# Rotary embedding: one signed sine product over eight positions on GpSimd, and one kind of TensorE tile

## Chip, cores and metric

The kernel runs on one core of a Trainium2 chip. The metric is the device time of one execution in microseconds (us). Times come from unprofiled runs. The profile is one more execution, recorded by the hardware profiler; its span, from the first to the last instruction, is a little shorter than the time.

## The reference

```python
batch, seq_len, n_heads, d_head = 8, 2048, 8, 64          # x is float32, 33.6 MB
def reference(x, cos, sin):                               # cos, sin: [2048, 32]
    x1 = x[..., :32]
    x2 = x[..., 32:]
    cos = cos[None, :, None, :]
    sin = sin[None, :, None, :]
    out1 = x1 * cos - x2 * sin
    out2 = x1 * sin + x2 * cos
    return np.concatenate([out1, out2], axis=-1)
```

Every row of 64 numbers (one head at one position) is split into halves of 32. Each half is multiplied by the cosines of its position, and to it is added the *other* half times the sines, with a minus sign for the first half. So out = x * cos + swap(x) * (-sin, +sin).

## The kernel before

A batch is laid out as 128 partitions with 16 positions each; a position is 8 heads of 64 numbers, that is HD = 512 elements. A batch is 4 MB in SBUF, there are five such buffers, and results are written in place before they are stored. The work goes in tiles of four positions (UNIT = 2048 elements), with halves of that at the very start and end. There are three kinds of tile:

- A: GpSimd multiplies by the sines (two instructions, one per half), VectorE multiplies by the cosines and adds.
- B: the same products, but TensorE adds them in PSUM, by multiplying both with the identity, and ScalarE copies the sum out.
- C: VectorE makes both products, without GpSimd; TensorE adds them (with the negative identity for the sign).

```python
    t1_pool = ctx.enter_context(tc.tile_pool(name="t1p", bufs=1, space=PSUM))
    o_pool = ctx.enter_context(tc.tile_pool(name="op", bufs=1, space=PSUM))
    t1s_pool = ctx.enter_context(tc.tile_pool(name="t1s", bufs=2))
    xpool = ctx.enter_context(tc.tile_pool(name="xpool", bufs=NBUF))     # NBUF = 5
    t2_pool = ctx.enter_context(tc.tile_pool(name="t2p", bufs=3))
    # ... tables: cos_sb, sin_sb, nsin in SBUF, cos_ps, sin_ps in PSUM ...
    for b, kind in ((1, "C"), (2, "B"), (3, "C"), (4, "B"), (5, "B")):
        kinds[(b, 0)] = kind                     # first tile of the batch; all others are "A"

    def rotate(b, lo, n):
        # ... t1 in PSUM for kind A, in SBUF (t1s) for B and C; t2 in SBUF ...
        if kind != "C":
            for u, tab in ((1, sin_sb), (0, nsin)):
                keep(nc.gpsimd.tensor_mul(
                        out=t2u[:, :, u, :].rearrange("p (r h) d -> p r h d", h=H),
                        in0=xu[:, :, 1 - u, :].rearrange("p (r h) d -> p r h d", h=H),
                        in1=rep(tab[:, r0 : r0 + nr, :], H)))
        keep(nc.vector.tensor_mul(out=t1..., in0=xk, in1=rep(cos_ps[...], 2 * H)))
        if kind == "A":
            keep(nc.vector.tensor_add(out=xt, in0=t1, in1=t2))
        elif kind == "B":
            for j in range(n // (2 * C)):        # C = 512
                o = o_pool.tile([P, 2 * C], f32, tag="o")
                for k in range(2):
                    # ... cs, oc: 512 columns of the tile and of o ...
                    nc.tensor.matmul(oc, eye, t1[:, cs], start=True, stop=False)
                    nc.tensor.matmul(oc, eye, t2[:, cs], start=False, stop=True)
                keep(nc.scalar.copy(xt[:, 2 * j * C : 2 * (j + 1) * C], o))
        else:
            # ... kind C: a second VectorE product with sin_ps, matmuls with eye and neye ...

    def pieces(b):
        if b == 0:    return [2 * HD, 2 * HD, UNIT, UNIT, UNIT]
        if b == last: return [UNIT, UNIT, UNIT, 2 * HD, 2 * HD]
        return [UNIT] * 4
    def shares(b):                               # what one store covers
        if b == 0:    return [HD, 7 * HD, 2 * UNIT]
        if b == last: return [2 * UNIT, UNIT, UNIT]
        return [ROW]
    # for each batch: rotate the pieces, store each share when it is done, then load batch b + 5
```

Loads are issued from the SyncE queue and stores from the ScalarE queue; those of the last batch go through SyncE too.

Of the kernel before, what the change touches and what calls it, by code (L numbers as in the profile page):

```python
# [9 lines left out]
@with_exitstack  # L10
def kernel(
    ctx: ExitStack,
    tc: tile.TileContext,
    x: bass.AP,
    cos: bass.AP,
    sin: bass.AP,
    out: bass.AP,
):
    nc = tc.nc
    keep = tc.keep_in_program_order  # L20
    f32 = mybir.dt.float32
    PSUM = bass.MemoryType.PSUM

    B, S, H, D = x.shape
    Dh = D // 2
    P = 128
    HD = H * D
    R = S // P
    ROW = R * HD
    UNIT = 4 * HD  # L30
    NBUF = 5
    C = 512
    last = B - 1

    xv = x.rearrange("b (q r) h d -> b q (r h d)", q=P)
    ov = out.rearrange("b (q r) h d -> b q (r h d)", q=P)
    cos_src = cos.rearrange("(q r) d -> q r d", q=P)
    sin_src = sin.rearrange("(q r) d -> q r d", q=P)

    const_pool = ctx.enter_context(tc.tile_pool(name="const", bufs=1))  # L40
    tab_pool = ctx.enter_context(tc.tile_pool(name="tab", bufs=1, space=PSUM))
    t1_pool = ctx.enter_context(tc.tile_pool(name="t1p", bufs=1, space=PSUM))
    o_pool = ctx.enter_context(tc.tile_pool(name="op", bufs=1, space=PSUM))
    t1s_pool = ctx.enter_context(tc.tile_pool(name="t1s", bufs=2))
    xpool = ctx.enter_context(tc.tile_pool(name="xpool", bufs=NBUF))
    t2_pool = ctx.enter_context(tc.tile_pool(name="t2p", bufs=3))

    cos_sb = const_pool.tile([P, R, Dh], f32, tag="cb")
    sin_sb = const_pool.tile([P, R, Dh], f32, tag="sb")
    nsin = const_pool.tile([P, R, Dh], f32, tag="ns")  # L50
    eye = const_pool.tile([P, P], f32, tag="eye")
    neye = const_pool.tile([P, P], f32, tag="neye")
    cos_ps = tab_pool.tile([P, R, Dh], f32, tag="cp")
    sin_ps = tab_pool.tile([P, R, Dh], f32, tag="sp")

    xts = {}

    def spans(sizes):
        lo = 0
        for n in sizes:  # L60
            yield lo, n
            lo += n

    def load(b):
        xt = xpool.tile([P, ROW], f32, tag="xt", name=f"xt{b}")
        for lo, n in spans([UNIT, UNIT, 2 * UNIT] if b == 0 else [ROW]):
            keep(nc.sync.dma_start(out=xt[:, lo : lo + n], in_=xv[b, :, lo : lo + n]))  # L67
            if b == 0 and lo == 0:
                keep(nc.sync.dma_start(out=cos_sb, in_=cos_src))  # L69
                keep(nc.sync.dma_start(out=sin_sb, in_=sin_src))  # L70
        xts[b] = xt

    def store(b, lo, n):
        queue = nc.sync if b == last else nc.scalar
        keep(queue.dma_start(out=ov[b, :, lo : lo + n], in_=xts[b][:, lo : lo + n]))  # L75

    for b in range(NBUF):
        load(b)

    nc.gpsimd.memset(eye, 0.0)  # L80
    nc.gpsimd.affine_select(
        out=eye,
        in_=eye,
        compare_op=mybir.AluOpType.not_equal,
        fill=1.0,
        base=0,
        pattern=[[-1, P]],
        channel_multiplier=1,
    )
    keep(nc.scalar.mul(nsin, sin_sb, -1.0))  # L90
    keep(nc.scalar.copy(sin_ps, sin_sb))  # L91
    keep(nc.scalar.mul(neye, eye, -1.0))
    keep(nc.vector.tensor_copy(cos_ps, cos_sb))  # L93

    def rep(a, n):
        return dataclasses.replace(a, ap=[a.ap[0][:], a.ap[1][:], [0, n], a.ap[-1][:]])

    kinds = {}
    for b, kind in ((1, "C"), (2, "B"), (3, "C"), (4, "B"), (5, "B")):
        kinds[(b, 0)] = kind  # L100

    def rotate(b, lo, n):
        kind = kinds.get((b, lo), "A")
        xt = xts[b][:, lo : lo + n]
        r0 = lo // HD
        nr = n // HD
        xk = xt.rearrange("p (r k d) -> p r k d", r=nr, d=Dh)
        xu = xt.rearrange("p (g u d) -> p g u d", u=2, d=Dh)
        if kind == "A":
            t1 = t1_pool.tile([P, n], f32, tag="t1")  # L110
        else:
            t1 = t1s_pool.tile([P, n], f32, tag="t1s")
        if kind == "C":
            t2 = t1s_pool.tile([P, n], f32, tag="t1s")
        else:
            t2 = t2_pool.tile([P, n], f32, tag="t2")
        t1u = t1.rearrange("p (g u d) -> p g u d", u=2, d=Dh)
        t2u = t2.rearrange("p (g u d) -> p g u d", u=2, d=Dh)
        if kind != "C":
            for u, tab in ((1, sin_sb), (0, nsin)):  # L120
                keep(
                    nc.gpsimd.tensor_mul(  # L122
                        out=t2u[:, :, u, :].rearrange("p (r h) d -> p r h d", h=H),
                        in0=xu[:, :, 1 - u, :].rearrange("p (r h) d -> p r h d", h=H),
                        in1=rep(tab[:, r0 : r0 + nr, :], H),
                    )
                )
        keep(
            nc.vector.tensor_mul(  # L129
                out=t1.rearrange("p (r k d) -> p r k d", r=nr, d=Dh),  # L130
                in0=xk,
                in1=rep(cos_ps[:, r0 : r0 + nr, :], 2 * H),
            )
        )
        if kind == "A":
            keep(nc.vector.tensor_add(out=xt, in0=t1, in1=t2))  # L136
        elif kind == "B":
            for j in range(n // (2 * C)):
                o = o_pool.tile([P, 2 * C], f32, tag="o")
                for k in range(2):  # L140
                    cs = slice((2 * j + k) * C, (2 * j + k + 1) * C)
                    oc = o[:, k * C : (k + 1) * C]
                    nc.tensor.matmul(oc, eye, t1[:, cs], start=True, stop=False)  # L143
                    nc.tensor.matmul(oc, eye, t2[:, cs], start=False, stop=True)  # L144
                keep(nc.scalar.copy(xt[:, 2 * j * C : 2 * (j + 1) * C], o))  # L145
        else:
            keep(
                nc.vector.tensor_mul(  # L148
                    out=t2.rearrange("p (r k d) -> p r k d", r=nr, d=Dh),
                    in0=xk,  # L150
                    in1=rep(sin_ps[:, r0 : r0 + nr, :], 2 * H),
                )
            )
            G = C // Dh
            for u in range(2):
                o = o_pool.tile([P, n // 2], f32, tag="o")
                for j in range(n // 2 // C):
                    oc = o[:, j * C : (j + 1) * C]
                    gs = slice(j * G, (j + 1) * G)
                    nc.tensor.matmul(oc, eye, t1u[:, gs, u, :], start=True, stop=False)  # L160
                    nc.tensor.matmul(  # L161
                        oc, eye if u else neye, t2u[:, gs, 1 - u, :], start=False, stop=True
                    )
                keep(
                    nc.scalar.copy(  # L165
                        xu[:, :, u, :], o.rearrange("p (g d) -> p g d", d=Dh)
                    )
                )

    def pieces(b):  # L170
        if b == 0:
            return [2 * HD, 2 * HD, UNIT, UNIT, UNIT]
        if b == last:
            return [UNIT, UNIT, UNIT, 2 * HD, 2 * HD]
        return [UNIT] * 4

    def shares(b):
        if b == 0:
            return [HD, 7 * HD, 2 * UNIT]
        if b == last:  # L180
            return [2 * UNIT, UNIT, UNIT]
        return [ROW]

    for b in range(B):
        done = 0
        outs = list(spans(shares(b)))
        for lo, n in spans(pieces(b)):
            rotate(b, lo, n)
            done = lo + n
            while outs and sum(outs[0]) <= done:  # L190
                store(b, *outs.pop(0))
        if b + NBUF <= last:
            load(b + NBUF)
# [30 lines left out]
```

## Time and profile before

| | |
|---|---|
| time, median of 3 runs | 163.48 us (163.35 to 163.52) |
| span of the profile | 161.6 us |
| VectorE busy | 140.1 us (87%), 66 instructions |
| GpSimd busy | 139.0 us (86%), 70 instructions |
| TensorE busy | 47.2 us (29%), 80 matmul passes |
| ScalarE busy | 12.8 us (8%) |
| moved by DMA | 67.65 MB, 419 GB/s over the span |

Busy time counts the stretches in which an engine worked; it does not say that the engine set the time. For that one reads which wait ended last: the profile notes, for each idle stretch of an engine, what released it, and it follows the work that ended last back through its releasers (the chain). "L122" is line 122 of the kernel: GpSimd's products are on L122, VectorE's cosine products on L129 and its adds on L136, the matmuls of kind B on L143 and L144 and their copies on L145. Queue q1 is that of SyncE, q10 that of ScalarE. In a line of the timeline, the first number is the start and the second the length in us; the brackets hold the idle time before, and what ended it.

### The profile page before, as it was taken

How to read it: one execution, taken by the hardware profiler on the slowest of the kernel's cores; microseconds unless marked ns; L12 is line 12 of the kernel's file. 1: busy time of each engine (PE TensorE's matmuls, PEld its weight loads, DVE VectorE, ACT ScalarE, POOL GpSimd, SP SyncE). 2: the span in 40 equal slices, each digit the busy share in tenths (PEclk: the TensorE clock that was granted, in tenths of full speed). 3: DMA queues.
4: the chain of work that ended last, by engine and by line, in shares of the span. 5: the costliest groups of instructions: out<-in, count | busy, mean ns of one | idle time of the engine just before them, and what ended most of it. 6: DMA issues, size and time to landing. Idle time of an engine off the chain costs nothing.

```text
span 161.6 us, 460 instructions
## 1 busy us (share of the span) xinstructions
PE 47.2 (29%) x80; PEld 17.8 (11%) x80; DVE 140.1 (87%) x66; ACT 12.8 (8%) x14; POOL 139.0 (86%) x70
## 2 busy tenths in 40 slices
PE   0000000497208760878029752972000000000000
PEld 0000000133003210222014211330000000000000
DVE  0468899999999999999999999999899998999900
ACT  3200000002200220021000220022000000000000
POOL 1299999999999899999996999998999969999200
PEclk9999999999965997599855998799555555555555
DMA  5999998899999999999999999999999999999995
GB/s 183 414 442 467 424 472 373 373 430 503 398 389 454 454 454 389 471 438 389 471 438 389 454 456 389 446 454 398 446 448 406 446 446 406 446 446 430 385 414 215
DMA packets 3458, 67.65 MB, mean 419 GB/s; under 512 B 384, under 2 KB 384, under 8 KB 768
## 3 DMA queue, kind: packets, MB, share of 16 engines
q1 hardware_dynamic: 2160, 38.27, 55.8%
q10 hardware_dynamic: 1296, 29.36, 42.2%
q14 instruction: 2, 0.02, 0.0%
HBM read 34.08 MB, written 33.55 MB: 419 GB/s over the span
## 4 chain that ended last, share of the span: by engine, by line
DMA 46%; DVE 37%; POOL 9%; issue 2%; SPq 1%; DVEq 0%; POOLq 0%; ACTq 0%
DMA xt<-in_x_dram 24%; DVE t L129 18%; DMA out_dram<-xt 18%; DVE xt L136 17%; POOL t L122 9%; DMA sin_sb<-in_sin_dram 3%; DVE t L148 1%; SPq L69 0%; SPq L67 0%; DVEq L136 0%; POOLq L122 0%; ACTq L75 0%
## 5 line engine op out<-in xcount | busy, mean ns | idle before, releaser
L122 POOL TENSOR_TENSOR t<-xt,sin_sb 128x1024 f32<-128x1024 f32 (+1 forms) x32 | 70.5, 2204 | 10.8 <-DMA sin_sb<-in_sin_dram 5.8
L129 DVE TENSOR_TENSOR t<-xt,cos_ps 128x2048 f32<-128x2048 f32 (+1 forms) x34 | 73.4, 2166 | 0.8
L122 POOL TENSOR_TENSOR t<-xt,nsin 128x1024 f32<-128x1024 f32 (+1 forms) x32 | 70.5, 2203 | 0.0
L136 DVE TENSOR_TENSOR xt<-t,t 128x2048 f32<-128x2048 f32 (+1 forms) x29 | 62.2, 2144 | 6.1 <-POOL t L122 3.7
L143 PE MATMUL o<-t,eye 128*128 128x512 f32 x24 | 16.5, 778 | 23.7 <-DVE t L129 20.2
L160 PE MATMUL o<-t,eye 128*128 128x512 f32 x16 | 10.6, 749 | 39.1 <-DVE t L129 36.9
L144 PE MATMUL o<-t,eye 128*128 128x512 f32 x24 | 14.7, 701 | 0.0
L145 ACT COPY xt<-o 128x1024 f32<-128x1024 f32 x6 | 6.1, 1012 | 45.7 <-PE o L144 45.7
L143 PEld LDWEIGHTS o<-t,eye 128*128 128x128 f32 x24 | 5.3, 244 | 32.8 <-issue 26.8
L160 PEld LDWEIGHTS o<-t,eye 128*128 128x128 f32 x16 | 3.6, 247 | 44.5 <-POOL t L122 30.6
L165 ACT COPY xt<-o 128x1024 f32<-128x1024 f32 x4 | 4.0, 1012 | 47.1 <-PE o L161 47.1
L144 PEld LDWEIGHTS o<-t,eye 128*128 128x128 f32 x24 | 5.7, 239 | 8.0 <-issue 8.0
L93 DVE COPY cos_ps<-cos_sb 128x512 f32<-128x512 f32 x1 | 0.7, 695 | 6.3 <-DMA cos_sb<-in_cos_dram 6.3
L161 PE MATMUL o<-t,neye 128*128 128x512 f32 x8 | 6.0, 847 | 0.2 <-DVE t L148 0.2
L148 DVE TENSOR_TENSOR t<-xt,sin_ps 128x2048 f32<-128x2048 f32 x2 | 4.6, 2279 | 0.0
L161 PE MATMUL o<-t,eye 128*128 128x512 f32 x8 | 4.1, 592 | 0.0
L161 PEld LDWEIGHTS o<-t,neye 128*128 128x128 f32 x8 | 1.8, 251 | 4.3 <-issue 2.7
L161 PEld LDWEIGHTS o<-t,eye 128*128 128x128 f32 x8 | 1.5, 190 | 1.9 <-issue 1.9
L90 ACT ACT_TABLE_LOAD x1 | 1.3, 1283 | 0.7 <-PEq L208 0.7
L90 ACT ACTIVATE nsin<-sin_sb 128x512 f32<-128x512 f32 x1 | 0.6, 630 | 5.0 <-DMA sin_sb<-in_sin_dram 5.0
L91 ACT COPY sin_ps<-sin_sb 128x512 f32<-128x512 f32 x1 | 0.6, 579 | 0.0
L80 POOL MEMSET eye<- 128x128 f32 x1 | 0.2, 205 | 0.3 <-POOLq L208 0.3
(6 smaller groups left out, 1.0 us busy)
## 6 DMA issues: line engine op xcount, KB each, us to landing
xt<-in_x_dram SPq DMA_DIRECT2D x7, 4096.0 KB, 39.0
out_dram<-xt ACTq DMA_DIRECT2D x6, 4096.0 KB, 28.3
xt<-in_x_dram SPq DMA_DIRECT2D x2, 1024.0 KB, 6.1
xt<-in_x_dram SPq DMA_DIRECT2D x1, 2048.0 KB, 11.5
out_dram<-xt ACTq DMA_DIRECT2D x1, 2048.0 KB, 25.3
out_dram<-xt SPq DMA_DIRECT2D x1, 2048.0 KB, 12.3
out_dram<-xt SPq DMA_DIRECT2D x2, 1024.0 KB, 8.7
out_dram<-xt ACTq DMA_DIRECT2D x1, 1792.0 KB, 20.2
```

Source lines behind the costliest of these rows:

```text
L90: keep(nc.scalar.mul(nsin, sin_sb, -1.0))
L93: keep(nc.vector.tensor_copy(cos_ps, cos_sb))
L122: nc.gpsimd.tensor_mul(out=t2u[:, :, u, :].rearrange("p (r h) d -> p r h d", h=H), in0=xu[:, :, 1 - u, :].rearrange("p (r h) d -> p r h d" ...
L129: nc.vector.tensor_mul(out=t1.rearrange("p (r k d) -> p r k d", r=nr, d=Dh), in0=xk, in1=rep(cos_ps[:, r0 : r0 + nr, :], 2 * H),)
L136: keep(nc.vector.tensor_add(out=xt, in0=t1, in1=t2))
L143: nc.tensor.matmul(oc, eye, t1[:, cs], start=True, stop=False)
L144: nc.tensor.matmul(oc, eye, t2[:, cs], start=False, stop=True)
L145: keep(nc.scalar.copy(xt[:, 2 * j * C : 2 * (j + 1) * C], o))
L148: nc.vector.tensor_mul(out=t2.rearrange("p (r k d) -> p r k d", r=nr, d=Dh), in0=xk, in1=rep(sin_ps[:, r0 : r0 + nr, :], 2 * H),)
L160: nc.tensor.matmul(oc, eye, t1u[:, gs, u, :], start=True, stop=False)
L161: nc.tensor.matmul(oc, eye if u else neye, t2u[:, gs, 1 - u, :], start=False, stop=True)
L165: nc.scalar.copy(xu[:, :, u, :], o.rearrange("p (g d) -> p g d", d=Dh))
```

## The change

The sine product becomes one GpSimd instruction instead of two: its first operand reads the two halves of each row in reversed order (a step of -32), and its second operand is a table `sgn` that holds -sin and +sin side by side for each position. One such instruction covers eight positions (4096 elements) in most batches, two to eight in the first, eight or four in the last. VectorE then works in tiles of four positions as before. Kind C is gone: in batches 1 to 5 the first four positions are added by TensorE in the manner of kind B, and all sine products are made by GpSimd. This needs fewer instructions and one code path, and takes two products off VectorE. The buffers change with it: t2 has two buffers of eight positions where it had three of four, t1s one buffer where it had two, and the negative identity and the sine table in PSUM are gone.

```diff
-    t1s_pool = ctx.enter_context(tc.tile_pool(name="t1s", bufs=2))
+    t1s_pool = ctx.enter_context(tc.tile_pool(name="t1s", bufs=1))
-    t2_pool = ctx.enter_context(tc.tile_pool(name="t2p", bufs=3))
+    t2_pool = ctx.enter_context(tc.tile_pool(name="t2p", bufs=2))
 ...
+    loads = {0: [4, 4, 8]}
+    products = {0: [2, 2, 4, 8], last: [8, 4, 4]}
+    stores = {0: [1, 7, 8], last: [8, 4, 4]}
+    on_tensor = {(b, 0) for b in range(1, 6)}
 ...
-    keep(nc.scalar.mul(nsin, sin_sb, -1.0))
-    keep(nc.scalar.copy(sin_ps, sin_sb))
-    keep(nc.scalar.mul(neye, eye, -1.0))
+    for lo, hi in ((0, 4), (4, R)):
+        keep(nc.scalar.mul(sgn[:, lo:hi, 0, :], sin_sb[:, lo:hi, :], -1.0))
+        keep(nc.scalar.copy(sgn[:, lo:hi, 1, :], sin_sb[:, lo:hi, :]))
 ...
+    def sine_product(b, lo, n):
+        xt = xts[b][:, lo * HD : (lo + n) * HD]
+        t2 = t2_pool.tile([P, n * HD], f32, tag="t2")
+        swapped = dataclasses.replace(
+            xt, offset=xt.offset + Dh,
+            ap=[xt.ap[0][:], [HD, n], [D, H], [-Dh, 2], [1, Dh]])
+        s = sgn[:, lo : lo + n, :, :]
+        signed = dataclasses.replace(
+            s, ap=[s.ap[0][:], [D, n], [0, H], [Dh, 2], [1, Dh]])
+        keep(nc.gpsimd.tensor_mul(out=t2..., in0=swapped, in1=signed))
+        return t2
 ...
+    def finish(b, lo, n, t2):
+        # ... t1 in SBUF (t1s) for tiles on_tensor, else in PSUM; cosine product as before ...
+        if (b, lo) not in on_tensor:
+            keep(nc.vector.tensor_add(out=xt, in0=t1, in1=t2))
+            return
+        # ... matmuls with eye and ScalarE copies exactly as in kind B ...
 ...
     for b in range(B):
-        for lo, n in spans(pieces(b)):
-            rotate(b, lo, n)
+        for lo, n in spans(products.get(b, [8, 8])):
+            t2 = sine_product(b, lo, n)
+            for at, m in spans([min(T, n)] * (n // min(T, n))):        # T = 4
+                finish(b, lo + at, m, t2[:, at * HD : (at + m) * HD])
 ...
```

## The prediction

> **What bounds the kernel now.** I began with the page's queue lines, because GpSimd at 86% and VectorE at 87% look like the limit and need not be.
>
> ```profile
> DMA packets 3458, 67.65 MB, mean 419 GB/s; under 512 B 384, under 2 KB 384, under 8 KB 768
> q1 hardware_dynamic: 2160, 38.27, 55.8%
> q10 hardware_dynamic: 1296, 29.36, 42.2%
> ```
>
> The two queues, loads and stores, together fill 98% of the 16 DMA engines' span of 161.6 us. The table of stretches of the span shows that this is true of every stretch but the first and the last (columns: stretch, length, then busy time of PE, PE load, VectorE, ScalarE, GpSimd, the granted clock, DMA share, GB/s):
>
> ```profile
> 0.00:5.00 5.00, 0.00 (x0) 0.00 (x0) 0.00 (x0) 1.28 (x1) 0.70 (x6) 1.00 0.64 218
> 5.00:45.00 40.00, 9.63 (x16) 3.49 (x16) 35.65 (x19) 3.38 (x5) 37.91 (x19) 1.00 1.01 429
> 125.00:155.00 30.00, 0.00 (x0) 0.00 (x0) 26.86 (x14) 0.00 (x0) 24.21 (x13) 0.50 0.99 427
> 155.00:162.00 7.00, 0.00 (x0) 0.00 (x0) 0.00 (x0) 0.00 (x0) 0.00 (x0) 0.50 0.65 275
> ```
>
> From 5 to 155 us the DMA share is about 1.00 at 427 to 435 GB/s. The chain of work that ended last agrees: in its middle it leaves the engines (columns: start, length, what):
>
> ```profile
> 63.12 29.40 DMA out_dram<-xt
> ...
> 92.59 39.11 DMA xt<-in_x_dram
> ...
> 131.83 4.63 POOL t L122 x2
> ...
> 152.18 1.22 DVE xt L136
> ```
>
> A store of batch 2 and the load of batch 7, which needs that store's buffer, hold 68.5 us of it. The last add ends at 153.4 us, the last 1 MB store is issued there and lands 7.3 us later, as older stores are still queued in front. So the kernel is bound by DMA, but VectorE and GpSimd are only a few us behind: a slowdown of theirs soon shows, a speedup hardly.
>
> **What the Trainium skill says.** DMA: Bandwidth & Descriptors (Specifications) gives a fabric ceiling of 435 GB/s; the trace's 427 to 435 in long stretches agrees. GPSIMD Engine Reference (3.1, Elementwise) puts a two-input operation at about 2.6 cycles per element at 1.2 GHz plus a dispatch per instruction: 2.17 ns per element; the trace gives 2.11 (below). SBUF — State Buffer (Who interferes with whom) says a VectorE instruction with at most one SBUF input does not contend with GpSimd; here the cosines and t1 of the adding tiles lie in PSUM, and GpSimd's spacing is 1.21 us at 8.32 with VectorE mostly idle and 1.20 at 9.53 with it at work: agreed, and unchanged by the change. TensorE: Matmul & The Clock Gate (What's actually happening) says the array starts at half clock and is let go after some 3.4 us of work; in this trace pairs of passes go from 2.04 to 1.02 us within a tile, each time anew.
>
> **The costs, from the timeline.** GpSimd, by the distance of starts:
>
> ```profile
> 8.32 1.25 POOL L122 TENSOR_TENSOR t<-xt,nsin 128x512 f32<-128x512 f32 x1
> 9.53 1.26 POOL L122 TENSOR_TENSOR t<-xt,sin_sb 128x512 f32<-128x512 f32 x1
> 46.27 2.33 POOL L122 TENSOR_TENSOR t<-xt,nsin 128x1024 f32<-128x1024 f32 x1
> 48.57 2.32 POOL L122 TENSOR_TENSOR t<-xt,sin_sb 128x1024 f32<-128x1024 f32 x1
> ```
>
> 512 elements take 1.21 us, 1024 take 2.28 (11.95 to 14.23) to 2.30 us. The slope is 1.08 us per 512 elements, which is one position, and the fixed part 0.13 us. One instruction over n positions then costs 0.13 + 1.08 n: 2.29 for two, 4.45 for four, 8.77 for eight. Four positions cost 4.58 today in two instructions. The new operand order walks the same runs of 32 elements on x, so I keep the slope.
>
> VectorE: an added tile of four positions has its pitch in the chain (product at 23.64, add at 26.04, before that add at 21.32): 2.40 + 2.32 = 4.72 us. A cosine product for a TensorE tile alone takes 2.2 us.
>
> One TensorE tile, first matmul to the second copy out:
>
> ```profile
> 100.06 2.04 PE L143 MATMUL o<-t,eye 128*128 128x512 f32 x2 [4.82 <-DVE t L129]
> ...
> 105.42 1.01 ACT L145 COPY xt<-o 128x1024 f32<-128x1024 f32 x1 [9.14 <-PE o L144]
> ...
> 110.23 1.01 ACT L145 COPY xt<-o 128x1024 f32<-128x1024 f32 x1 [3.79 <-PE o L144]
> ```
>
> TensorE lets go of t2 when the second copy starts: 10.2 us after its first matmul here, 10.0 in batch 2 (49.12 to 59.16), 11.5 in batch 4 (83.81 to 95.27); mean 10.6.
>
> **The change part by part.**
> - GpSimd's arithmetic. Before: 30 tiles of four positions, two of them in halves, 28 x 4.58 + 2 x 4.84 = 137.9 us; two more (batches 1 and 3) had their sine product on VectorE. After: all 32. Batch 0: 2.29 + 2.29 + 4.45 + 8.77 = 17.8; batches 1 to 6: 12 x 8.77 = 105.2; batch 7: 8.77 + 2 x 4.45 = 17.7. Sum 140.7, so +2.8 us: fewer instructions save about 6.4, the two tiles taken over cost 9.
> - VectorE loses two sine products and their second tiles (4.4 us) and the split of the last tile (0.5). Per batch from 1 to 5 it needs 2.2 + 3 x 4.72 = 16.4 us against GpSimd's 17.5, so it is off the path there; in batches 0, 6 and 7 it needs 18.9 and is on it.
> - Grain. An add can start only when a whole instruction is done: 8.77 us instead of 4.6 after the start of the product.
> - Buffers. Three t2 buffers of four positions become two of eight. The next but one product must wait until TensorE has let go of its tile. Call F the end of that product. GpSimd asks for the buffer at F + 8.77. VectorE finishes the group before (add, product, add) 7.0 after that group's end and then the cosine product, 2.2: about F + 0.5 without a stall, earlier by s after a stall of s. TensorE needs 10.6 from there, so it is done near F + 11.2 - s, and the new stall is 2.4 - s. This swings about 1.2 us, once for each of batches 2 to 6: 6.0 us.
> - Setup. The signed table takes two ScalarE passes after sine lands at 6.97, some 0.3 us each for four positions (the pass over 128x128 took 0.30): the first product starts at about 7.65 instead of 7.09.
>
> **The sum.** Batch 6 starts on GpSimd at 7.65 + 17.8 + 10 x 8.77 + 6.0 = 119.2 (before: 112.33). Its first product is done at 127.9 (first add before: 116.97). Then eight tiles of four on VectorE without a gap: 7 x 4.72 + 2.3 = 35.3, so the last add ends at 163.2 (before 153.4). Loads do not hold this up: before, x of batches 4 to 7 landed by 73.1, 92, 112.3 and 131.8, and here those batches start near 80, 100, 119 and 137. Stores: those of batches 1 to 5 go out 4 to 11 us later than before, DMA runs dry towards the end, and the last 1 MB store then takes about 5 us (the first 1 MB load took 4.9 with an empty queue). 168.2, plus 0.8 to the end of the span (as before, 160.8 to 161.6), plus the 1.9 us by which the time exceeds the span (163.48 against 161.6): 170.9. I take a little off for starts that overlap by about 0.1 us and predict **170.0 us**, 4.0% slower.
>
> **The rivals.**
> - DMA stays the bound and swallows it all: about 163.5. For it: the queues are full today, and no byte changes. Against: only some 5 us of the last store's wait is slack, and the sum adds 10 us at the last add. Faster by 2% would mean a span of about 158.3, and 67.65 MB at 435 GB/s take 155.5 without the 1.8 us before the first packet and the last receipt; nothing in the change speeds up a transfer.
> - TensorE's hold on t2 never stalls GpSimd, since its first matmul runs before the product is done or the clock is up early: the 6.0 goes, 164.9, within 2%. For it: the margin is small (10.6 against 8.77 + 0.5). Against: no tile before took under 10.0 us.
> - The long instruction has another rate. The reversed pair of halves and the zero step in one pattern have no example in this trace. 5% more per element is 0.43 us for each of sixteen groups, about 7 us, partly in place of the stalls: 174 to 177. If 5% less, VectorE and TensorE take over and it ends near 166.
> - VectorE's relief (4.9 us) decides: it would if it were the limit in the middle. It waited 3.7 us for GpSimd in all, so it was near it, but the product work moves to GpSimd, which becomes the slower of the two.
>
> **Range and chances.** Stalls of 0.5 to 2.0 us per batch instead of 1.2 move the end by -3.5 to +4.0, and the GpSimd rate by 2% moves it by about 3: 165.5 to 174.5. The line of 2% is at 166.75; only the first two rivals lie under it. Faster 0.03, same 0.22, slower 0.75.
>
> **What would show it.** GpSimd instructions over 4096 elements starting 8.7 to 8.9 us apart; a wait of GpSimd of 1 to 2 us before the first product of batches 2 to 6, put down to TensorE or the ScalarE copies; batch 6 starting near 119; VectorE without gaps from 128 to 163; the DMA share falling clearly under 1 after about 130 us, and the last store landing in about 5 us. Wrong would be: GpSimd without such waits, a first add of batch 6 before 122, or DMA still at 1.00 to the end.

## The result and the profile after

The changed kernel takes 195.24 us (194.78 to 196.25, 6 runs) against 163.49 us (163.35 to 163.68, 6 runs) for the kernel before, run beside it: a ratio of 1.195 (95% interval 1.191 to 1.198). The prediction was 170.0 us, in a range of 165.5 to 174.5: the direction was right, and the loss is almost five times the one predicted. In what follows, ratios leave disturbed runs out, so they can differ a little from the quotient of two medians.

The page of the changed kernel, its queue lines:

```profile
DMA packets 3457, 67.64 MB, mean 350 GB/s; under 512 B 384, under 2 KB 384, under 8 KB 768
q1 hardware_dynamic: 2160, 38.27, 47.5%
q10 hardware_dynamic: 1296, 29.36, 35.7%
```

The bytes are the same, but the queues fill only 83% of the span, where they filled 98%. The table of stretches (columns as in the prediction) says where the rest went. First the kernel before between 85 and 125 us, then the changed kernel:

```profile
85.00:125.00 40.00, 18.07 (x32) 6.78 (x30) 38.36 (x18) 4.05 (x4) 37.63 (x17) 0.76 1.00 431
...
85.00:125.00 40.00, 15.52 (x26) 5.28 (x25) 27.14 (x12) 3.04 (x3) 25.77 (x4) 0.73 1.00 427
125.00:155.00 30.00, 9.19 (x14) 3.27 (x14) 15.70 (x7) 2.02 (x2) 22.89 (x4) 0.67 0.53 226
155.00:185.00 30.00, 0.00 (x0) 0.00 (x0) 29.25 (x14) 0.00 (x0) 24.64 (x4) 0.50 0.50 201
```

Between 85 and 125 us DMA is as full as before, at 427 GB/s; from 125 to 185 us it stands at half: the last load was issued at 95.9 us, and DMA is idle between one store and the next. But the damage is done earlier: between 85 and 125 us VectorE works 27.1 of 40 us (before: 38.4) and GpSimd 25.8 (before: 37.6). Two engines that should overlap each stand idle a third of the time. The list of who waited for whom (columns: total us, times, longest):

```profile
DVE xt L138 <- POOL t L114: 44.8, 12, 6.6
...
POOL t L114 <- issue: 28.4, 4, 7.1
```

VectorE waits for products, as is natural. The second line is the one to stop at: GpSimd waits four times, 7.1 us each, and "issue" says that the profile found no releaser. The timeline of GpSimd shows where they lie:

```profile
45.16 17.68 POOL L114 TENSOR_TENSOR t<-xt,sgn 128x4096 f32<-128x4096 f32 x2 [1.99 <-PE o L146]
69.95 17.65 POOL L114 TENSOR_TENSOR t<-xt,sgn 128x4096 f32<-128x4096 f32 x2 [7.11 <-issue]
94.71 17.65 POOL L114 TENSOR_TENSOR t<-xt,sgn 128x4096 f32<-128x4096 f32 x2 [7.11 <-issue]
119.47 17.64 POOL L114 TENSOR_TENSOR t<-xt,sgn 128x4096 f32<-128x4096 f32 x2 [7.12 <-issue]
144.22 30.89 POOL L114 TENSOR_TENSOR t<-xt,sgn 128x4096 f32<-128x4096 f32 x4 [7.11 <-issue]
```

The waits of 7.1 us stand before the first product of batches 3, 4, 5 and 6; the one before batch 2 is 2.0 us and ends on TensorE. What VectorE does in the first of them, from the timeline of all engines:

```profile
53.98 8.86 POOL L114 TENSOR_TENSOR t<-xt,sgn 128x4096 f32<-128x4096 f32 x1
...
62.47 1.01 ACT L147 COPY xt<-o 128x1024 f32<-128x1024 f32 x1 [3.79 <-PE o L146]
62.87 2.29 DVE L138 TENSOR_TENSOR xt<-t,t 128x2048 f32<-128x2048 f32 x1 [3.60 <-POOL t L114]
65.20 2.29 DVE L131 TENSOR_TENSOR t<-xt,cos_ps 128x2048 f32<-128x2048 f32 x1
67.53 2.29 DVE L138 TENSOR_TENSOR xt<-t,t 128x2048 f32<-128x2048 f32 x1
...
69.95 17.65 POOL L114 TENSOR_TENSOR t<-xt,sgn 128x4096 f32<-128x4096 f32 x2 [7.11 <-issue]
78.82 2.29 DVE L138 TENSOR_TENSOR xt<-t,t 128x2048 f32<-128x2048 f32 x1 [4.60 <-POOL t L114]
```

The second product of batch 2 ends at 62.84. Add, product, add take VectorE until 69.82. Only then, at 69.95, does the first product of batch 3 begin. The next product starts exactly when the one *just made* has been read. TensorE has long been done with the older buffer: ScalarE's last copy of that tile starts at 62.47. So GpSimd writes again into the buffer that it filled last, though the other is free. The built programs bear this out: the first product of batch 3 stands behind a wait for VectorE's 25th instruction, which is the last add of batch 2. And this is the buffer, A or B, of each product in order.

```
batch                    0        1    2    3    4    5    6    7
changed kernel           A B A B  A B  A B  B A  A B  B A  A B  A B A
without TensorE tiles    A B A B  A B  A B  A B  A B  A B  A B  A B A
```

Between batches 2 and 3, 3 and 4, 4 and 5, 5 and 6, a letter repeats. The buffer is chosen when the program is built, not by the chip.

### The profile page after: what moved, and what is told of

It reads as the page before. It is cut to its first block, busy times and chain, and to the rows that moved or that the text cites. A ratio compares the mean times of both kernels' runs of the same rounds, so it can differ in the third digit from the quotient of the medians.

```text
span 193.0 us, 409 instructions
## 1 busy us (share of the span) xinstructions
PE 49.6 (26%) x80; PEld 18.1 (9%) x80; DVE 135.4 (70%) x62; ACT 12.7 (7%) x15; POOL 142.3 (74%) x25
## 5 line engine op out<-in xcount | busy, mean ns | idle before, releaser
L114 POOL TENSOR_TENSOR t<-xt,sgn 128x4096 f32<-128x4096 f32 (+2 forms) x19 | 141.6, 7481 | 40.7 <-issue 28.4
L145 PE MATMUL o<-t,eye 128*128 128x512 f32 x40 | 28.4, 800 | 75.1 <-DVE t L131 69.4
L146 PE MATMUL o<-t,eye 128*128 128x512 f32 x40 | 25.9, 737 | 13.9 <-POOL t L114 13.9
L145 PEld LDWEIGHTS o<-t,eye 128*128 128x128 f32 x40 | 8.9, 247 | 90.4 <-issue 45.0
L146 PEld LDWEIGHTS o<-t,eye 128*128 128x128 f32 x40 | 9.2, 239 | 29.3 <-POOL t L114 19.7
L99 DVE COPY cos_ps<-tabs 128x512 f32<-128x512 f32 x1 | 0.7, 694 | 6.2 <-DMA tabs<-in_cos_dram 6.2
L97 ACT ACTIVATE sgn<-tabs 128x128 f32<-128x128 f32 (+1 forms) x2 | 0.8, 414 | 5.0 <-DMA tabs<-in_sin_dram 5.0
L98 ACT COPY sgn<-tabs 128x128 f32<-128x128 f32 (+1 forms) x2 | 0.8, 388 | 0.0
```

The source lines that it names most:

```text
L97: keep(nc.scalar.mul(sgn[:, lo:hi, 0, :], sin_sb[:, lo:hi, :], -1.0))
L98: keep(nc.scalar.copy(sgn[:, lo:hi, 1, :], sin_sb[:, lo:hi, :]))
L114: nc.gpsimd.tensor_mul(out=t2.rearrange("p (r h u d) -> p r h u d", r=n, h=H, u=2), in0=swapped, in1=signed,)
```

## The experiments

The theory: at each of the four repeats GpSimd and VectorE work in turn and not side by side, and this costs 24 of the 32 us. Rivals: long instructions as such make the two engines alternate; TensorE's hold on t2 costs the time; the new operand order is slow.

**Buffers in turns.** Two tags with one buffer each, used alternately; nothing else is changed.

```diff
-        t2 = t2_pool.tile([P, n * HD], f32, tag="t2")                    # bufs=2
+        t2 = t2_pool.tile([P, n * HD], f32, tag=f"t2{next(turn) % 2}")   # bufs=1
```

Expected:

> Theory (the buffer choice): in the changed kernel the first sine product of batches 3 to 6 is written into the t2 buffer that the product just before it has filled, so GpSimd waits about 7.1 us, four times, until VectorE has read that product. Here the two buffers take turns by force and nothing else changes. The four waits vanish and waits of 1 to 2 us on TensorE remain: 195.2 - 28.4 + 4 x 1.5 = 173 us, within 168 to 176. Rival 1 (long instructions as such make GpSimd and VectorE alternate): stays above 190. Rival 2 (TensorE's hold on t2 costs the time): above 185.

Measured: 171.27 us, ratio 1.050 (1.044 to 1.057). GpSimd's timeline in this run:

```profile
45.40 35.32 POOL L117 TENSOR_TENSOR t<-xt,sgn 128x4096 f32<-128x4096 f32 x4 [2.25 <-PE o L149]
82.95 35.34 POOL L117 TENSOR_TENSOR t<-xt,sgn 128x4096 f32<-128x4096 f32 x4 [2.24 <-PE o L149]
120.51 30.91 POOL L117 TENSOR_TENSOR t<-xt,sgn 128x4096 f32<-128x4096 f32 x4 [2.22 <-PE o L149]
```

The four waits of 7.1 us are gone; three of 2.2 us on TensorE remain, at every second batch. 28.4 us of waits give way, less the 4.7 us by which the TensorE waits grow (6.7 against 2.0 in the changed kernel): 23.7, and the time falls by 24.0. Instructions, tiles and bytes are the same, so the first rival falls, and TensorE's hold is left with the 6.7 us.

**No TensorE tile.** `on_tensor` is empty; VectorE makes all adds.

```diff
-    on_tensor = {(b, 0) for b in range(1, 6)}
+    on_tensor = set()
```

Expected:

> The changed kernel with no TensorE tile: all adds on VectorE, t2 buffers free again in the order in which they were filled. Theory: no wait of 7.1 us on GpSimd; VectorE now sets the end: add of the long product of batch 0 at 25.5 us, then 30 tiles x 4.72 us less the first product = 165 us, 7 to 8 us to the end of the last store and of the time: 172, within 168 to 177. Rival 1 (long instructions as such): above 190. Rival 2 (TensorE's hold): also about 172, so e1 tells it from the theory.

Measured: 170.16 us, ratio 1.041 (1.038 to 1.043). With one tag and two buffers, as in the changed kernel, the products now take turns (the second row of letters), and GpSimd waits some 0.5 us per product for VectorE, which is the bound, as here:

```profile
79.47 8.85 POOL L114 TENSOR_TENSOR t<-xt,sgn 128x4096 f32<-128x4096 f32 x1 [0.52 <-DVE xt L138]
```

So giving VectorE *more* work (busy 147.8 us, against 135.4) made the changed kernel 25 us faster. It also shows what the build's own repeats need: the TensorE tile in the first product of a batch. Why the build then takes the newer buffer, and does not yet do so at batch 2, is not shown; I suppose that it reckons TensorE's part to end later than it does.

**Two repeats, and repeats without TensorE.** The buffer of each product is given by a list: once with the repeats of batches 3 and 4 alone, once with all four but without TensorE tiles.

```diff
+        order = "0101" "01" "01" "10" "01" "01" "01" "010"     # two repeats
+        order = "0101" "01" "01" "10" "01" "10" "01" "010"     # four, on_tensor = set()
-        ... tag=f"t2{next(turn) % 2}"
+        ... tag=f"t2{order[next(turn)]}"
```

Expected:

> The run with buffers in turns, but with the changed kernel's repeats of a buffer at batches 3 and 4 alone. Theory: each repeat costs the same, a wait of 7.1 us less the TensorE wait that it saves, (195.2 - 171.3) / 4 = 6.0 us: 171.3 + 12 = 183 us, within 180 to 186. Rival (slack in the DMA queues takes up the first repeats): under 177.

> The run without TensorE tiles (170.2 us), with the order of buffers of the changed kernel, so four repeats. Theory: the loss needs no TensorE tile, only the repeats; VectorE idles at each for 8.8 us of product less one cosine product of 2.3: 170.2 + 4 x 6.5 = 196 us, within 191 to 200. Rival (it is TensorE that makes the repeats dear): under 180.

Measured: 184.09 us for two repeats, ratio 1.127 (1.124 to 1.131), and 196.45 us for four without TensorE, ratio 1.203 (1.201 to 1.205). GpSimd's timeline with two repeats:

```profile
70.54 17.65 POOL L117 TENSOR_TENSOR t<-xt,sgn 128x4096 f32<-128x4096 f32 x2 [7.11 <-issue]
95.30 17.65 POOL L117 TENSOR_TENSOR t<-xt,sgn 128x4096 f32<-128x4096 f32 x2 [7.12 <-issue]
113.67 17.66 POOL L117 TENSOR_TENSOR t<-xt,sgn 128x4096 f32<-128x4096 f32 x2 [0.72 <-PE o L149]
133.79 8.83 POOL L117 TENSOR_TENSOR t<-xt,sgn 128x4096 f32<-128x4096 f32 x1 [2.46 <-PE o L149]
```

None, two and four repeats give 171.3, 184.1 and 195.2 us: some 6 us each, whether TensorE has a part in it or not (170.2 to 196.5 without it, 6.6 each). The loss follows the number of repeats, with TensorE tiles and without. No slack in the DMA queues took up the first of them.

**Half the instruction, same buffers.** Each product of eight positions is made by two instructions of four into the same buffer, with turns, and with the changed kernel's own choice of buffers.

```diff
-        keep(nc.gpsimd.tensor_mul(out=t2..., in0=swapped, in1=signed))          # n positions
+        for at in range(0, n, 4):
+            keep(nc.gpsimd.tensor_mul(out=t2[at : at + 4]..., in0=..., in1=...))
```

Expected:

> The run with buffers in turns (171.3 us), but each sine product of eight positions made by two instructions of four into the same buffer. Theory: what is left of the loss is the grain of the instruction: the first add of a product starts 4.4 us earlier, the cosine tile for TensorE is ready before its product, the waits of 2.2 us on TensorE go. DMA is the bound again: 164.5 us, within 163 to 167. Rival (what is left is the size of the buffers, TensorE holding eight positions for four): 169 to 172.

> The changed kernel with its own choice of buffers, each product of eight made by two instructions of four. Theory: GpSimd still waits four times for the product just made to be read, but VectorE is then only one add behind, so some 2.6 us each instead of 7.1: 172 us, within 168 to 177. Rival (the choice of buffer costs its 24 us whatever the grain): about 189 or more.

Measured: with turns 163.94 us, ratio 1.004 (1.001 to 1.006); with the repeats 173.42 us, ratio 1.062 (1.060 to 1.063). GpSimd's timeline in the latter:

```profile
64.24 17.96 POOL L116 TENSOR_TENSOR t<-xt,sgn 128x2048 f32<-128x2048 f32 x4 [2.87 <-DVE xt L150]
85.08 17.96 POOL L116 TENSOR_TENSOR t<-xt,sgn 128x2048 f32<-128x2048 f32 x4 [2.88 <-DVE xt L150]
105.92 17.97 POOL L116 TENSOR_TENSOR t<-xt,sgn 128x2048 f32<-128x2048 f32 x4 [2.88 <-DVE xt L150]
126.77 35.80 POOL L116 TENSOR_TENSOR t<-xt,sgn 128x2048 f32<-128x2048 f32 x8 [2.87 <-DVE xt L150]
```

The same four waits, in the same places, are now 2.9 us, and here the profile names their releaser: VectorE's add. With an instruction of four positions VectorE has done its first tile by the time the product is complete, so a repeat costs little more than one add (2.3 us); with one of eight it costs add, product and add. In the run with turns GpSimd has no wait after its first product:

```profile
7.53 143.64 POOL L119 TENSOR_TENSOR t<-xt,sgn 128x1024 f32<-128x1024 f32 x33 [6.23 <-ACT sgn L99]
```

So the 7.3 us between 171.27 and 163.94 are the grain of the instruction, and with the 24.0 us of the repeats they make 31.3 of the 31.8 us lost. The two are not independent: a repeat costs 6.0 us with the long instruction and (173.42 - 163.94) / 4 = 2.4 us with the short one, so that either cure alone wins most of the loss.

**Four buffers of four positions.** The changed kernel with products of four positions and four t2 buffers in turns, the same bytes.

```diff
-    products = {0: [2, 2, 4, 8], last: [8, 4, 4]}          # other batches [8, 8]
+    products = {0: [2, 2, 4, 4, 4]}                        # other batches [4, 4, 4, 4]
-        ... tag="t2"
+        ... tag=f"t2{next(turn) % 4}"
```

Expected:

> The changed kernel with sine products of four positions, in four t2 buffers of four positions that take turns; same bytes of buffer, same TensorE tiles. Theory: no long wait, the add can start 4.5 us after its product began, DMA is the bound again: 163 us, within 162 to 166. Rival 1: also about 163, so it doesn't tell those two apart; if it stays over 170, the grain and the choice of buffer are both not the cause.

Measured: 163.84 us, ratio 1.001 (0.999 to 1.002). VectorE is busy 135.4 us instead of 140.1, one kind of TensorE tile does instead of two, t1s still has one buffer, and the time is that of the kernel before.

**The kernel before with the one signed product.** GpSimd's two instructions per tile become one, with the signed table that it needs; tiles, kinds and t2 buffers stay.

```diff
-            for u, tab in ((1, sin_sb), (0, nsin)):
-                keep(nc.gpsimd.tensor_mul(out=t2u[:, :, u, :]..., in0=xu[:, :, 1 - u, :]..., in1=rep(tab...)))
+            keep(nc.gpsimd.tensor_mul(out=t2..., in0=swapped, in1=signed))
```

Expected:

> The kernel before with its two sine products per tile replaced by the one signed product, tiles, kinds and t2 buffers as before. Theory: the operand order costs nothing per element, GpSimd has 0.13 us less per tile, DMA is the bound: 163.5 us, within 0.5%. Rival 3 (the reversed halves or the zero step make the instruction slower): GpSimd spacing over 4.6 us for four positions and a time over 165.

Measured: 163.58 us, ratio 1.000 (0.999 to 1.002). GpSimd's timeline:

```profile
98.20 13.52 POOL L133 TENSOR_TENSOR t<-xt,sgn 128x2048 f32<-128x2048 f32 x3 [0.20 <-DVE xt L147]
```

Three products of four positions in 13.52 us are 4.5 us each, where two instructions took 4.58: here reversed halves and zero step cost nothing that shows.

**Only cosines.** No sine products, no adds, no TensorE; VectorE multiplies by the cosines in place. The sine half of the result is left out, and loads and stores are the same.

```diff
-            t2 = sine_product(b, lo, n)
-    ... out=t1, then add of t1 and t2
+    ... out=xt
```

Expected:

> The changed kernel without sine products, adds and TensorE: VectorE multiplies by the cosines in place, and the same loads and stores run. It leaves out the sine half of the result. Theory (67.65 MB through the DMA queues bound the kernel before and the good variants): 161 to 163.5 us although no engine is busy for half of the span. Rival (the engines bound the kernel before): under 158.

Measured: 162.97 us, ratio 0.996 (0.995 to 0.997). From its page, busy time by engine, and from its stretches (columns: stretch, length, VectorE, ScalarE, GpSimd, clock, DMA share, GB/s):

```profile
DVE 72.0 (45%) x34; ACT 2.6 (2%) x5; POOL 0.7 (0%) x6
```

```profile
85.00:125.00 40.00, 18.18 (x9) 0.00 (x0) 0.00 (x0) 1.00 1.00 433
125.00:155.00 30.00, 8.88 (x4) 0.00 (x0) 0.00 (x0) 1.00 0.99 425
```

Without GpSimd's products and with half of VectorE's work, 0.5 us are won. So with these loads and stores the arithmetic had hardly anything to give, and no arrangement tried here gained over the kernel before.

## Why the prediction was right or wrong

**The bound before** was right: the queues are the limit, and a relief of the engines gains nothing (1.001 with VectorE's 4.7 us less, 1.000 with one GpSimd instruction per tile, 0.996 with half of VectorE's work and no products on GpSimd).

**GpSimd's arithmetic** was right: 8.77 us predicted for eight positions, 8.82 measured (starts at 45.16 and 53.98); the first product at 7.65 predicted, 7.62 measured. **VectorE's relief**, 4.9 us, measured 4.7.

**Buffers** is the step that failed: "The next but one product must wait until TensorE has let go of its tile." It supposes that two buffers take turns. In the changed kernel, four times out of the five in which I reckoned a TensorE wait, the very next product waited, for VectorE, 7.1 us: 28.4 us on VectorE and 2.0 us on TensorE in place of my 6.0 us on TensorE. For a kernel whose buffers do take turns the sum was good: 170.0 predicted, 171.27 measured; the first add of batch 6 at 127.9, measured 129.38; and the swing of "the new stall is 2.4 - s" is there, as waits of 2.25, none, 2.24, none, 2.22, or 6.7 us.

The profile of the kernel before held the sign, and I had read past it. In its timeline, fourth product of batch 2:

```profile
51.29 2.29 DVE L136 TENSOR_TENSOR xt<-t,t 128x2048 f32<-128x2048 f32 x1
...
53.66 2.33 POOL L122 TENSOR_TENSOR t<-xt,sin_sb 128x1024 f32<-128x1024 f32 x1 [0.46 <-DVE xt L136]
...
59.16 1.01 ACT L145 COPY xt<-o 128x1024 f32<-128x1024 f32 x1 [3.79 <-PE o L144]
```

With three buffers in turn, this product would take the buffer of the first of the batch, which TensorE reads until 59.1. It starts at 53.66, as soon as the *second* tile has been added. So buffers were not in turns there either. There this was even the better choice, as the buffer whose turn it was stayed busy for 5.4 us longer; the repeat cost 0.5 us here and 1.5 us in batch 4, in a kernel whose DMA queues were full.

**Grain** was right as a mechanism and its size close: 8.77 us to the first add of a product. What I had not separated is that it also feeds the TensorE stall; halving the instruction takes both away, 7.3 us.

**DMA at the end** was right in kind: it runs dry after 125 us, and the two last stores of 1 MB land in 4.5 us on average, the very last in 3.8 (5 predicted). **The rivals**: none of the four had two engines working in turn; all varied the size of terms in a pipeline whose shape I took as given. The direction was not luck: with buffers in turns, as I had them, the kernel is still 5.0% slower. The range was too narrow, as it held only errors of size.

## What to carry to other kernels

With a pool of two buffers, do not assume which one the next tile gets: look in the trace at which reader each wait of the writer ends on, and force turns by separate tags where overlap depends on it. Larger instructions save a fixed cost (here 0.13 us each) and pay for it in latency to the first reader and in the price of every buffer wait. And before making engines faster, run the transfers with little else: here that would have shown that half of VectorE's work and all of GpSimd's products were worth 0.4%.

## What was not expected of the hardware

A wait can appear in the profile without a releaser: the 7.1 us waits are put down to "issue", though the built program waits for VectorE's add there, and with the instruction halved the waits in the same places are put down to that add. So "issue" on an engine that has work can be a wait, and is to be looked into. DMA kept 425 to 433 GB/s from 5 to 155 us with VectorE at half of its work and GpSimd idle (the run with cosines only) and 427 to 435 with all of them at work: here engine work took nothing from the transfers.
